# One layer of a diffusion backbone with a mixture of experts on Trainium2: a bias table with memory of its own, one modulation chunk later, a place table ahead of a gate

## The chip, the cores and the metric

The kernel runs on one core of one Trainium2 chip. The metric is device time in microseconds (us), the median of repeated executions. Engines are named as in the profile: PE (TensorE matmul), PEld (its weight load), DVE (VectorE), ACT (ScalarE), POOL (GpSimd), SP (SyncE, which here only issues transfers). A name with q (ACTq, SPq) is an engine's instruction queue.

## The reference

One layer over 256 latent tokens and 256 context tokens of width 1024, all in float32. What matters here:

```python
mod = split((silu(c) @ w_ada + b_ada), 6)                 # w_ada is 1024 x 6144
h = modulate(rms_norm(x), mod[0], mod[1])
y = token_mixing(h, hc, ...) @ w_o                        # windowed GQA and latent attention
x = x + mod[2] * rms_norm(y)
h2 = modulate(rms_norm(x), mod[3], mod[4])
logits = h2 @ w_router + b_router                         # 32 experts, the best 4 of each token
...
gate, lin = split(xb @ w_gate_up[e] + b_gate_up[e], 2)    # 1024 x 2048 per expert
act = (min(gate, 7) * sigmoid(1.702 * gate)) * (clip(lin, -7, 7) + 1)
ys = act @ w_down[e] + b_down[e]                          # 1024 x 1024 per expert
out[token] += weight[token, e] * ys
x = x + mod[5] * rms_norm(out)
```

Every expert's weights are read once: 32 experts of 12 MB.

## The kernel before

The program has three stages. **Projections**: modulation, norms and the input projections. **Attention**: eight units of two heads, written out by hand as a list of calls. **Experts**: a loop over 32 experts. From attention on, each engine carries out its instructions in the order in which the program was written, so a line of that list sets the order on PE, DVE, ACT, POOL and on the queue of SP at once.

*Weight slots.* A slot holds 128 x 2048 float32 (1024 KB). SP loads into slots in a fixed order: the four remaining column groups of `w_ada` in 16 chunks (`ada_load`, L418, source `in_wadr`), `w_o` in four (`load_wo`, L582, `in_wo`), and then 12 slots for each expert (`load`, L743, `in_wexp`): 0 to 3 and 4 to 7 for the two halves of gate and up, 8 to 11 for down. In the expert loop 18 slots take turns. Each transfer signals its landing on one of eight semaphores, which take turns; a transfer may be issued only when the one that used its semaphore before has landed, and when its slot has been read. So about eight transfers are in flight.

*Ada chunks.* `ada(1)` issues the next chunk's load and then does the oldest loaded chunk: two DVE instructions (L431, `accw<-slot,silu,accw`, 128 x 1024) that add two rows of `w_ada`, scaled, to a sum. That chunk's slot is then free for the load. Four chunks make one modulation vector; `accw_106` is the one that the router's shift needs (`column(1)`, L612).

*Attention's calls that the change passes.* `weights(u)` computes scores (L686) and their exponentials (ACT L695); its sums over keys are POOL's (`adds`, L701 and L702, `pa<-pT`). `k_mid` copies keys (ACT L529, L530), `k_flip` transposes them on PE (L536, into the two PSUM buffers `tp`), and each `tp` is split in two: ACT writes the rounded part (L137, `kTm`), DVE the rest (L138, `kTl`). `q_up`, `v_up`, `q_flip` do the same for queries (`qTm`) and values; `v_split` keeps one slot until the last `v_up`. `top_b` finds row maxima (PE L635, DVE L636, `mx`), `values` multiplies by the values (PE L710), `mix(k)` by `w_o` (PE L726, `y`): `mix(0)` and `mix(1)` read what `load_wo(0)` loaded, `mix(2)` and `mix(3)` that of `load_wo(1)`.

*Experts.* Tokens of two experts are gathered by matmuls with a 0/1 table (`take`, PE L995, then `xg`, ACT L1007). `G_(e,c,ks)` multiplies them by half of gate or up (PE L1028, `pw<-slot,xg`; a half in two parts, LOW and HIGH, of two slots each); `T_` transposes the result (PE L1041, `pf`) and makes the activation on DVE and ACT (L1046 to L1053, `actT`); `D_` multiplies by the down weights (PE L1028, `pw<-slot,actT`); `scatter` adds the output to the tokens (PE L1058, `acc`). `place` makes the table that `scatter` uses: two DVE or POOL instructions (L1019, `wo_`), two PE transposes (L1021, `px<-con,wo_`) and an ACT copy (L1022, `ctt`); its `wo_` buffers are single.

*The bias of the down products.* In the loop's turn for expert 30, `bias_rows()` takes a buffer of the tag `xg` (shared with the gathered tokens) and lets ACT issue the load of `b_down` (L1083, `bd<-in_bdn`, 128 KB); `bias_flip` transposes the token weights; and after `G_(31, 0, LOW)`, `bias_add` multiplies the two into the sums (PE L1094, `acc<-bd,wT`, four matmuls). The order there is:

```python
G_(e, 1, HIGH)          # e = 30
bd = bias_rows(); bias_flip(0); bias_flip(1)
G_(31, 0, LOW)
bias_add(0, bd); bias_add(1, bd)
T_(e, 1); G_(31, 0, HIGH); D_(e, LOW); T_(31, 0); D_(e, HIGH)
```

After the last scatter, `finish` normalises, adds and stores the output.

Of the kernel before, what the change touches and what calls it, by code (L numbers as in the profile page):

```python
# [7 lines left out]
F32 = mybir.dt.float32  # L8
# [11 lines left out]
D = 1024  # L20
# [3 lines left out]
E = 32  # L24
# [46 lines left out]
def layer_kernel(ctx, tc, x, cx, cc, wadr, bada, grows, win0, winB, winC, winD, wuqa, wuqb, wukv, wo, wr, wexp, bgu, bgx, bdn, cols, rows, consts, out):  # L71
    nc = tc.nc
    V, S, G, PE = nc.vector, nc.scalar, nc.gpsimd, nc.tensor
# [10 lines left out]
    def wide():  # L84
        return ring.tile([P, 2048], F32, name="slot", tag="wide", bufs=2)
# [50 lines left out]
    def split(hi, lo, src, late=False, eng=V):  # L136
        a = S.copy(hi, src)  # L137
        b = eng.tensor_tensor(lo, src, hi.bitcast(F32), op=ALU.subtract)  # L138
        if late:
            tc.keep_in_program_order(a)  # L140
            tc.keep_in_program_order(b)
# [26 lines left out]
    def ptp(shape=(P, 4, P)):  # L168
        return psb.tile(list(shape), F32, name="tp", tag="tp", bufs=2)
# [240 lines left out]
    def ada_load(pool=None):  # L410
        ch, s = divmod(ada_n[0], 4)
        ada_n[0] += 1
        if s == 0:
            G.memset(accs[ch], 0.0)
            nc.sync.dma_start(accs[ch][0:1], bada[ch:ch + 1])
        w = slot() if pool is None else pool.tile([P, 2048], F32, name="ax", tag="ax", bufs=1)
        w = w.rearrange("p (k c) -> p k c", c=D)
        nc.sync.dma_start(w, wadr[8 + ch * 4 + s].rearrange("p (k c) -> p k c", c=D))  # L418
        ada_q.append((ch, s, w))

    def ada_do(n=1):
        for _ in range(n):
            ch, s, w = ada_q.pop(0)
            a = accs[ch]
            for k in range(2):
                sk = silu[:, 2 * s + k, 0:1]
                if (ch, s, k) in ADA_G:
                    S.activation(w[:, k], w[:, k], AF.Copy, scale=sk)
                    G.tensor_tensor(a, a, w[:, k], op=ALU.add)
                else:  # L430
                    V.scalar_tensor_tensor(a, w[:, k], sk, a, op0=ALU.mult, op1=ALU.add)  # L431
# [95 lines left out]
    def k_mid(i):  # L527
        k96[i] = pqa.tile([P, 8, 96], F32, name="k96", tag="ct", bufs=2)
        S.copy(k96[i][:, :, 0:64], pk[i].rearrange("p (h d) -> p h d", h=8))  # L529
        S.copy(k96[i][:, :, 64:96], krt[:, i][:, None].to_broadcast([P, 8, 32]))  # L530
# [22 lines left out]
    def q_flip(n, t):  # L553
        pt = ptp((96, 4, P))
        for j in range(4):
            PE.transpose(pt[:, j], q96[n, t][:, j], ident)
        split(qTm[n][0:96, 0, t], qTm[n][0:96, 1, t], pt)
# [22 lines left out]
    def load_wo(i):  # L580
        w = wide()
        nc.sync.dma_start(w, wo[i])  # L582
        for k in range(2):
            wov[2 * i + k] = w[:, k * 1024:(k + 1) * 1024]
# [46 lines left out]
    def top_b(h):  # L631
        n, j = divmod(h, 4)
        for t in range(NT):
            s_ = pmm((P, 512))
            PE.matmul(s_, qTm[n][0:96, 0, t, j], kTm[0][n][0:96, j], start=True, stop=True)  # L635
            V.tensor_reduce(mxs[n][:, t, j:j + 1], s_, axis=AX.X, op=ALU.max)  # L636
# [26 lines left out]
    def weights(u):  # L663

        a = u < 4
        pT_[u] = [av.tile([P, 4, T], F32, name="pT", bufs=4) for h in range(2)]
        for g in range(2):
            st = [pmm((P, 2, T)) for h in range(2)]
            for kk in range(2):
                kt = 2 * g + kk  # L670
                ks = slice(kt * P, (kt + 1) * P)
                ops = []
                for h in range(2):
                    if a:
                        k_ = [x_[HALF[h], ks] for x_ in kTg]
                        q_ = [x_[HALF[h], :, u] for x_ in qTg]
                        sl, r = sel[HALF[h], u], rows_["a"][HALF[h]]
                    else:
                        n, j = divmod(2 * (u - 4) + h, 4)
                        k_ = [x_[n][0:96, j, ks] for x_ in kTm]  # L680
                        q_ = [qTm[n][0:96, i, :, j] for i in range(2)]
                        sl, r = sel[0:96, j], rows_[n][0:96]
                    ops.append([(k_[0], q_[0]), (k_[0], q_[1]), (k_[1], q_[0]), (sl, r)])
                for i in range(4):
                    for h in range(2):
                        PE.matmul(st[h][:, kk], *ops[h][i], start=(kk == 0 and i == 0), stop=(i == 3 and not (a and g)),  # L686
                                  skip_group_check=True)
                if a and g:
                    t = 3 - kt
                    for c in range(2):  # L690
                        for h in range(2):
                            PE.matmul(st[h][:, kk, t * P + c * 64:t * P + c * 64 + 64], mask_s[HALF[h], t, c],
                                      ident_b[HALF[h], HALF[h]], start=False, stop=True, skip_group_check=True)
            for h in range(2):
                S.activation(pT_[u][h][:, 2 * g:2 * g + 2], st[h], AF.Exp, scale=A_SCALE if a else B_SCALE)  # L695
        adds(u)
# [34 lines left out]
    tag = {"b0": "big0", "b1": "big1", "d0": "held0", "d1": "held1", "d2": "held2"}  # L731
# [13 lines left out]
    def ada(n):  # L745
        for _ in range(n):
            if ada_n[0] < 16:
                ada_load()
            if ada_q:
                ada_do()  # L750
# [11 lines left out]
    ada(1)  # L762
    weights(0)
    k_mid(0)
    ada(1)
    weights(1)
    k_flip(3)
    k_mid(1)
# [20 lines left out]
    v_up(3)  # L789
    load_wo(0)  # L790
    q_flip(1, 1)
    load_wo(1)
    top_b(0)
    open_y()
# [171 lines left out]
    mo = ctx.enter_context(tc.tile_pool(name="mo", bufs=2, reuse_waits="tile"))  # L966
# [63 lines left out]
    def pw_tile():  # L1030
        return pm.tile([P, 512], F32, name="pw", tag="pw", bufs=2)
# [6 lines left out]
    def flip_z(gu):  # L1038
        pf = pm.tile([P, 4, 2, CAP], F32, name="pf", tag="pf", bufs=1)
        for b in range(4):  # L1040
            PE.transpose(pf[:, b].rearrange("p h c -> p (h c)"), gu[:, b * P:(b + 1) * P], ident)  # L1041
        return pf
# [17 lines left out]
    def act_tile():  # L1060
        return mo.tile([P, KD, CAP], F32, name="actT")
# [6 lines left out]
    def pre(p, eng=G, oh=None):  # L1068
        es = (2 * p, 2 * p + 1)
        g = Gather([(lambda t, e=e: posm[t][:, e:e + 1], lambda t, e=e: wtr[t][:, e:e + 1]) for e in es], eng, oh)  # L1070
        for i, e in enumerate(es):
            gs2[e] = (g, i)
        return g
# [4 lines left out]

    wTs = {}

    def bias_rows():
        bd = mo.tile([E, D], F32, name="bd", tag="xg")
        S.dma_start(bd, bdn)  # L1083
        return bd

    def bias_flip(t):
        px = px_tile().rearrange("p k c -> p (k c)")
# [1 line left out]
        wTs[t] = mo.tile([E, P], F32, name="wT")  # L1089
        V.tensor_copy(wTs[t], px[0:E, 0:P])  # L1090

    def bias_add(t, bd):
        for n in range(2):
            PE.matmul(acc[t][n], wTs[t], bd[:, n * 512:(n + 1) * 512], start=False, stop=False, skip_group_check=True)  # L1094

    g0 = pre(0, V, oh0)
# [41 lines left out]
    def T_(e, c):  # L1138
        if c == 0:
            acts[e] = act_tile()  # L1140
        swiglu(flip_z(gus.pop((e, c))), bg[:, e, c], acts[e], c)

    def D_(e, ks):
        if ks[0] == 0:
            pts[e] = pw_tile()
        gemm(pts[e], wsl(e, 8), lambda k: acts[e][:, k], ks)
        if ks[-1] == KD - 1:
            ys[e] = evict(pts.pop(e), "y")
# [8 lines left out]
    for e in range(E):  # L1157
        loads(12 * e + 12)
        nxt = e + 1 < E
        if e == 0:  # L1160
            G_(0, 1, LOW)
            T_(0, 0)
            G_(0, 1, HIGH)
            G_(1, 0, LOW)
            T_(0, 1)
            G_(1, 0, HIGH)
            g0.place(0)
            D_(0, LOW)
            T_(1, 0)
            g0.place(1)  # L1170
            D_(0, HIGH)
            continue
        g = gs2[e][0] if e % 2 == 0 else pre((e + 1) // 2) if nxt else None
        step = [g.place, g.place] if e % 2 == 0 else [g.take, g.take] if nxt else None
        if step:
            step[0](0)
        G_(e, 1, LOW)
        if step:
            step[1](1)
        if e:  # L1180
            scatter(ys.pop(e - 1), gs2[e - 1][0].ctt[gs2[e - 1][1]], e == 1)
        G_(e, 1, HIGH)
        if e == E - 3:
            count()
        if e == E - 2:
            bd = bias_rows()
            for t in range(NT):
                bias_flip(t)
        if nxt:
            G_(e + 1, 0, LOW)  # L1190
        if e == E - 2:
            for t in range(NT):
                bias_add(t, bd)
        T_(e, 1)
        if nxt:
            G_(e + 1, 0, HIGH)
        D_(e, LOW)
        if nxt:
            T_(e + 1, 0)
        D_(e, HIGH)  # L1200
# [190 lines left out]
```

## Time and profile before

| | |
|---|---|
| median of 3 runs | 1219.4 us (1218.92 to 1219.73) |
| the profiled execution's own time | 1215.98 us |
| its span, first to last instruction | 1214.2 us |
| PE busy | 1107.7 us (91% of the span) |
| DVE, ACT, POOL busy | 306.0, 231.6, 131.7 us |
| moved by DMA | 446.58 MB, 368 GB/s over the span |
| issued loads of expert weights | 384 of 1024 KB, median 19.9 us from issue to landing |
| chain of work that ended last | DMA 64%, PE 30%, DVE 4% of the span |

All times in the rows below are microseconds from the span's start. A busy share over the whole span is a mean over three stages with different limits; which one decides is read stage by stage. A row of the timeline gives start, length, engine, line, operation, output and inputs, the count of instructions merged, and in brackets how long the engine stood idle before it and what ended that.

### The profile page before, as it was taken

How to read it: one execution, taken by the hardware profiler on the slowest of the kernel's cores; microseconds unless marked ns; L12 is line 12 of the kernel's file. 1: busy time of each engine (PE TensorE's matmuls, PEld its weight loads, DVE VectorE, ACT ScalarE, POOL GpSimd, SP SyncE). 2: the span in 40 equal slices, each digit the busy share in tenths (PEclk: the TensorE clock that was granted, in tenths of full speed). 3: DMA queues.
4: the chain of work that ended last, by engine and by line, in shares of the span. 5: the costliest groups of instructions: out<-in, count | busy, mean ns of one | idle time of the engine just before them, and what ended most of it. 6: DMA issues, size and time to landing. Idle time of an engine off the chain costs nothing.

```text
span 1214.2 us, 13597 instructions
## 1 busy us (share of the span) xinstructions
PE 1107.7 (91%) x5441; PEld 474.7 (39%) x5441; DVE 306.0 (25%) x651; ACT 231.6 (19%) x509; POOL 131.7 (11%) x186
## 2 busy tenths in 40 slices
PE   7799899999999999999898989898989898989575
PEld 1587557643343343433232323232323232323121
DVE  3785778431111111121111111111111111111012
ACT  3534412311111111111111111111111111111001
POOL 0301514100101101010101010101010101010000
PEclk9899999899999999999999999999999999999869
DMA  9750386889999999999999999999999999999950
GB/s 380 294 178 1 105 357 232 363 350 420 421 420 420 420 420 420 420 420 420 421 420 421 420 420 420 421 420 419 420 420 421 421 419 421 420 420 421 420 228 36
DMA packets 63194, 446.58 MB, mean 368 GB/s; under 512 B 7284, under 2 KB 7540, under 8 KB 10008
## 3 DMA queue, kind: packets, MB, share of 16 engines
q1 hardware_dynamic: 62648, 444.24, 88.9%
q10 hardware_dynamic: 480, 1.44, 0.4%
q8 instruction: 44, 0.72, 0.2%
q14 instruction: 22, 0.18, 0.0%
HBM read 444.60 MB, written 1.05 MB: 367 GB/s over the span
## 4 chain that ended last, share of the span: by engine, by line
DMA 64%; PE 30%; DVE 4%; ACT 1%; issue 1%; POOL 0%; SPq 0%; POOLq 0%; DVEq 0%; ACTq 0%
DMA slot<-in_wexp 63%; PE pw L1028 11%; PE y L726 2%; PE mm L686 2%; PE mm L274 2%; PE mm L710 1%; PE mm L148 1%; PE mm L146 1%; PE mm L147 1%; PE acc L1058 1%; DVE accw L431 1%; PE px L995 1%; PE pr L547 1%; PE pf L1041 1%; PE acc L1094 1%
## 5 line engine op out<-in xcount | busy, mean ns | idle before, releaser
L1028 PE MATMUL pw<-slot,xg 128*64 128x512 f32 x2048 | 469.5, 601 | 17.5 <-DMA slot<-in_wexp 17.5
L1028 PE MATMUL pw<-slot,actT 128*64 128x512 f32 x1024 | 243.5, 604 | 26.5 <-DMA slot<-in_wexp 25.0
L1028 PEld LDWEIGHTS pw<-slot,xg 128*64 128x64 f32 x2048 | 137.2, 137 | 299.7 <-issue 240.1
L1046 DVE TENSOR_TENSOR z<-pf,bg 128x512 f32<-128x512 f32 x64 | 44.2, 691 | 756.8 <-PE pf L1041 756.8
L1028 PEld LDWEIGHTS pw<-slot,actT 128*64 128x64 f32 x1024 | 69.1, 137 | 176.6 <-issue 104.3
L1050 ACT ACTIVATE sg<-z 128x256 f32<-128x256 f32 x64 | 26.7, 417 | 340.2 <-DVE z L1048 340.2
L1035 ACT COPY gu<-pw 128x512 f32<-128x512 f32 x64 | 37.5, 586 | 229.9 <-PE pw L1028 229.9
L995 PEld LDWEIGHTS px<-oh,xt 128*128 128x128 f32 x480 | 55.8, 191 | 24.3 <-issue 24.3
L1058 PE MATMUL acc<-y,ctt 64*128 64x512 f32 x256 | 63.6, 615 | 0.7 <-ACT y L1035 0.7
L995 PE MATMUL px<-oh,xt 128*128 128x128 f32 x480 | 61.5, 281 | 0.0
L1007 ACT ACTIVATE xg<-px,vcol 128x128 f32<-128x128 f32 x120 | 45.2, 457 | 80.8 <-PE px L995 80.8
L1041 PEld LDWEIGHTS pf<-con,gu 128*128 128x128 f32 x256 | 27.1, 141 | 53.4 <-issue 51.8
L1041 PE MATMUL pf<-con,gu 128*128 128x128 f32 x256 | 42.4, 289 | 0.7 <-ACT gu L1035 0.7
L1035 ACT COPY y<-pw 128x512 f32<-128x512 f32 x32 | 18.8, 586 | 92.5 <-PE pw L1028 89.2
L985 POOL TENSOR_SCALAR oh<-con,posm,r 128x64 f32<-128x64 f32 x60 | 34.0, 586 | 2.5 <-DVE posm L925 2.5
L1052 DVE TENSOR_TENSOR sg<-z,sg 128x256 f32<-128x256 f32 x64 | 27.2, 425 | 18.0 <-ACT sg L1050 18.0
L701 POOL TENSOR_TENSOR pa<-pT 128x512 f32<-128x512 f32 x16 | 23.1, 1447 | 69.3 <-ACT pT L695 54.8
L1058 PEld LDWEIGHTS acc<-y,ctt 64*128 64x128 f32 x256 | 22.0, 186 | 21.8 <-issue 18.4
L726 PE MATMUL y<-slot,of 128*128 128x512 f32 x64 | 30.4, 617 | 0.1
L1053 DVE SCALAR_TENSOR_TENSOR actT<-z,sg 128x256 f32<-128x256 f32 x64 | 27.2, 425 | 2.2
L1094 PE MATMUL acc<-bd,wT 32*128 32x512 f32 x8 | 7.2, 1072 | 21.0 <-DMA bd<-in_bdn 21.0
L274 PE MATMUL mm<-slot,siluz 128*4 128x512 f32 x40 | 19.4, 635 | 7.5 <-DMA slot<-in_wadr 7.5
(449 smaller groups left out, 879.1 us busy)
## 6 DMA issues: line engine op xcount, KB each, us to landing
slot<-in_wexp SPq DMA_DIRECT2D x384, 1024.0 KB, 19.9
slot<-in_wadr SPq DMA_DIRECT2D x20, 1024.0 KB, 7.3
ax<-in_wadr SPq DMA_DIRECT2D x4, 1024.0 KB, 5.8
slot<-in_wo SPq DMA_DIRECT2D x4, 1024.0 KB, 6.3
slot<-in_win SPq DMA_DIRECT2D x2, 1024.0 KB, 9.6
slot<-in_winD SPq DMA_DIRECT2D x2, 768.0 KB, 9.1
slot<-in_winB SPq DMA_DIRECT2D x2, 576.0 KB, 5.5
ct<-in_cx SPq DMA_DIRECT2D x2, 512.0 KB, 10.9
```

The source lines that it names most:

```text
L274: PE.matmul(pad[ch][n], siluz[:, 2 * s + k], w[:, k, n * 512:(n + 1) * 512], start=(s == 0 and k == 0), stop=(last and k == 1), skip_group ...
L726: PE.matmul(y[t][n], oT[k][:, t * P:(t + 1) * P], wov[k][:, n * 512:(n + 1) * 512], start=(k == 0), stop=(k == KD - 1), skip_group_check=True)
L985: eng.tensor_scalar(oh[t][:, i], iota[:, 0:CAP], pos_ap(t), r2[t], op0=ALU.is_equal, op1=ALU.mult)
L995: PE.matmul(px[:, k, 0:ne * CAP], xt[t][:, kk * P:(kk + 1) * P], self.oh[t][:, 0:ne].rearrange("p e c -> p (e c)"), start=(k == 0 and t == ...
L1007: S.activation(o, i, AF.Identity, scale=vcol[:, 1, kk:kk + 1], bias=vcol[:, 0, kk:kk + 1])
L1028: PE.matmul(pt[HALF[h]], lhs(k), wk(k, h), start=(k == 0), stop=(k == KD - 1), skip_group_check=True)
L1035: S.copy(y, pt)
L1041: PE.transpose(pf[:, b].rearrange("p h c -> p (h c)"), gu[:, b * P:(b + 1) * P], ident)
L1046: V.tensor_tensor(z, pf, bias[:, :, :, None].to_broadcast([P, 4, 2, CAP]), op=ALU.add)
L1052: V.tensor_tensor(sg, zg, sg, op=ALU.mult)
L1053: V.scalar_tensor_tensor(actT[:, 4 * c:4 * c + 4], zl, 1.0, sg, op0=ALU.add, op1=ALU.mult)
L1058: PE.matmul(acc[t][n], ctt[HALF[n], t], y[HALF[n]], start=begin, stop=last, skip_group_check=True)
```

## The change

Three edits in the order of the program. The load of `b_down` moves out of the loop to the head of the expert stage, into a tile of its own. One `ada(1)` moves from between `k_mid(0)` and `weights(1)` to between the two `load_wo` calls. In the first expert's turn `g0.place(1)` goes ahead of `T_(1, 0)`.

```diff
     weights(0)
     k_mid(0)
-    ada(1)
     weights(1)
     k_flip(3)
...
     load_wo(0)
     q_flip(1, 1)
+    ada(1)
     load_wo(1)
     top_b(0)
...
-    def bias_rows():
-        bd = mo.tile([E, D], F32, name="bd", tag="xg")
-        S.dma_start(bd, bdn)
-        return bd
+    bd = mo.tile([E, D], F32, name="bd", bufs=1)
+    S.dma_start(bd, bdn)
...
-    def bias_add(t, bd):
+    def bias_add(t):
...
             D_(0, LOW)
+            g0.place(1)
             T_(1, 0)
-            g0.place(1)
             D_(0, HIGH)
...
         if e == E - 2:
-            bd = bias_rows()
             for t in range(NT):
                 bias_flip(t)
```

On DVE in attention, where `k_flip(2)` and then `k_flip(3)` split their transposes, and later where `q_flip(1, 1)` ends and `top_b(0)` begins (rows of before with -, of the change with +):

```order
 L138 TENSOR_TENSOR kTl_1024<-tp,kTm_1022 96x4x128
 L138 TENSOR_TENSOR kTl_1025<-tp,kTm_1023 96x4x128
-L431 SCALAR_TENSOR_TENSOR accw_106<-slot,silu,accw_106 128x1024 x4
+L431 SCALAR_TENSOR_TENSOR accw_106<-slot,silu,accw_106 128x1024 x2
 L138 TENSOR_TENSOR kTl_1024<-tp,kTm_1022 96x4x128
 L138 TENSOR_TENSOR kTl_1025<-tp,kTm_1023 96x4x128
...
 L138 TENSOR_TENSOR qTm_1027<-tp,qTm_1027 96x512 x2
+L431 SCALAR_TENSOR_TENSOR accw_106<-slot,silu,accw_106 128x1024 x2
 L636 TENSOR_REDUCE mx<-mm 128x1 x4
 L431 SCALAR_TENSOR_TENSOR accw_107<-slot,silu,accw_107 128x1024 x2
```

Two of the four chunk instructions ahead of the second `kTl` pair now stand ahead of the first row maxima. On the queue of SP the chunk loads keep their number, but the second of the two loads that stood ahead of the `w_o` loads now stands between them:

```order
 L418 DMA slot<-in_wadr 128x2048 x2
 L415 DMA accw_107<-in_bada 1x1024
-L418 DMA slot<-in_wadr 128x2048 x2
-L582 DMA slot<-in_wo 128x2048 x2
+L418 DMA slot<-in_wadr 128x2048
+L582 DMA slot<-in_wo 128x2048
+L418 DMA slot<-in_wadr 128x2048
+L582 DMA slot<-in_wo 128x2048
 L418 DMA slot<-in_wadr 128x2048
 L743 DMA slot_1571<-in_wexp 128x2048
```

On ACT at the head of the expert stage, now (bg is the table of the gate and up biases; in brackets the semaphores that an instruction waits for, DMAHW0 to DMAHW7 being the eight of the transfers):

```order
L888 COPY h2T_2035<-mm 128x512 [waits PE_49]
L971 DMA bg<-in_bgu 128x512 [waits DMAHW7_49,PE_49]
L1082 DMA bd<-in_bdn 32x1024 [waits DMAHW5_49,DMAHW0_49]
L1007 ACTIVATE xg<-acc_2229,vcol 128x128 [waits PE_49]
L1007 ACTIVATE xg<-acc_2229,vcol 128x128 x3
```

and before, in the turn of expert 30:

```order
L1035 COPY gu<-pw 128x512 [waits PE_49,Activation_49]
L1083 DMA bd<-in_bdn 32x1024 [waits DMAHW6_49]
L1050 ACTIVATE sg<-z 128x256 [waits DVE_49]
L1035 COPY gu<-pw 128x512 [waits PE_49,Activation_49]
```

The load of bd went from behind an eviction of expert 30 to behind the load of bg, ahead of the first gathered tokens.

## Rows read from the trace of the kernel before

**Rows 1.** Windows: length, busy PE, PEld, DVE, ACT, POOL; PE clock; DMA share; GB/s.

```profile
252.00:257.00 5.00, 5.00 (x26) 1.59 (x24) 2.80 (x13) 0.81 (x5) 0.00 (x0) 1.00 0.64 221
...
264.00:371.00 107.00, 104.24 (x504) 39.45 (x500) 17.12 (x45) 17.96 (x41) 9.11 (x16) 0.98 1.01 421
...
371.00:1135.00 764.00, 719.78 (x3410) 261.50 (x3410) 106.85 (x266) 115.35 (x261) 57.87 (x101) 1.00 1.01 420
...
1135.00:1165.00 30.00, 8.63 (x28) 2.82 (x25) 0.56 (x2) 0.59 (x1) 0.00 (x0) 0.65 1.01 413
```

**Rows 2.** The chain that ended last: start, length, what.

```profile
1135.86 19.87 DMA slot<-in_wexp
...
1155.74 5.64 DMA bd<-in_bdn
...
1200.73 0.02 issue
```

**Rows 3.** The same windows view, the microsecond in which the transfers end.

```profile
1173.00:1174.00 1.00, 1.00 (x6) 0.33 (x4) 0.00 (x0) 0.00 (x0) 0.00 (x0) 0.50 0.02 8
```

**Rows 4.** Timeline of PE round the bias matmuls.

```profile
1136.77 3.65 PE L1028 MATMUL pw<-slot,xg 128*64 128x512 f32 x16
...
1161.43 7.19 PE L1094 MATMUL acc<-bd,wT 32*128 32x512 f32 x8 [21.00 <-DMA bd<-in_bdn]
...
1169.59 6.17 PE L1028 MATMUL pw<-slot,xg 128*64 128x512 f32 x16
...
1179.12 0.66 PE L1041 MATMUL pf<-con,gu 128*128 128x128 f32 x4
...
1186.72 1.99 PE L1058 MATMUL acc<-y,ctt 64*128 64x512 f32 x8
```

**Rows 5.** Timeline of DVE, ACT and PE in attention.

```profile
121.36 7.38 DVE L431 SCALAR_TENSOR_TENSOR accw<-slot,silu,accw 128x1024 f32<-128x1024 f32 x4
...
125.11 1.12 ACT L137 CAST kTm<-tp 96x512 fp32r<-96x512 f32 x2
...
129.40 1.53 PE L536 MATMUL tp<-con,k 128*96 128x128 f32 x8 [4.35 <-DVE kTl L138]
...
130.86 3.29 PE L710 MATMUL mm<-pT,vg 128*64 128x256 f32 x16
...
143.73 1.95 PE L710 MATMUL mm<-pT,vg 128*64 128x256 f32 x16
```

**Rows 6.** The windows view, two microseconds of attention behind a wait of PE.

```profile
132.00:134.00 2.00, 2.00 (x14) 1.07 (x12) 0.27 (x1) 0.00 (x0) 0.00 (x0) 0.59 0.45 184
```

**Rows 7.** Timeline of DVE where the chunk goes.

```profile
166.41 1.29 DVE L636 TENSOR_REDUCE mx<-mm 128x1 f32<-128x512 f32 x2 [1.97 <-PE mm L635]
...
167.62 2.60 DVE L431 SCALAR_TENSOR_TENSOR accw<-slot,silu,accw 128x1024 f32<-128x1024 f32 x2
...
173.25 2.48 DVE L636 TENSOR_REDUCE mx<-mm 128x1 f32<-128x512 f32 x4 [0.91 <-PE mm L635]
```

**Rows 8.** Timeline of SP's queue and of PE, loads and use of w_o.

```profile
154.65 1.01 SPq L582 DMA_DIRECT2D slot<-in_wo  x2
...
161.46 0.33 SPq L418 DMA_DIRECT2D slot<-in_wadr  x1
...
175.80 3.68 PE L726 MATMUL y<-slot,of 128*128 128x512 f32 x8
```

**Rows 9.** Timeline of PE in the first expert's turn.

```profile
280.13 0.30 PE L1021 MATMUL px<-con,wo__2403 128*128 128x128 f32 x1 [2.76 <-DVE wo__2403 L1019]
...
280.52 5.27 PE L1028 MATMUL pw<-slot,actT 128*64 128x512 f32 x16
```

**Rows 10.** Timeline of ACT's and SP's queues at the expert stage's head.

```profile
203.94 17.87 SPq L743 DMA_DIRECT2D slot<-in_wexp  x10
...
246.06 0.34 ACTq L971 DMA_DIRECT2D bg<-in_bgu  x1
...
250.64 1.51 ACT L1007 ACTIVATE xg<-acc,vcol 128x128 f32<-128x128 f32 x4 [8.46 <-PE acc L995]
```

More of the change, by code (lines that the diff above doesn't have):

```diff
@@ L1192, in layer_kernel @@
             for t in range(NT):
-                bias_add(t, bd)
+                bias_add(t)
         T_(e, 1)
```

## The prediction

> **What bounds the kernel now.** I read the windows by stage first. From 264 to 1165 us the transfers run at 413 to 421 GB/s with a DMA share of 1.01, in every stretch [rows 1]; just ahead of that, at 252 to 257, they reach 221 GB/s. A slot of 1,048,576 bytes takes 2.5 us at 420 GB/s. So from 264 on the stream of weights is full: when it ends is settled by when it became full and by the bytes left. PE follows it: in 371 to 1135 it is busy 719.78 of 764.00 us and waits for weights the rest. The reader should see that a faster PE buys nothing there.
>
> Next I read the end of the chain of waits. It leaves the weights at 1155.72, when one load lands; at once ACT issues the load of bd, which takes 5.64 us, and from its landing on the chain is PE's [rows 2]. The timeline of PE shows what that is: PE ends a gate half at 1140.42, stands idle for 21.00 us until bd is there, and then needs 7.19 us for the bias matmuls [rows 4], while the stream goes on at 413 GB/s [rows 1]. Finer windows show the stream's end: 8 GB/s in 1173 to 1174 [rows 3], so the last slot landed at about 1173.9. The last down matmul ends at 1200.73 [rows 2] and the span at 1214.2: PE ends 27 us behind the weights. Those 27 us are the price of one wait.
>
> **Term 1, bd's wait.** ACT's last work ahead of that issue is an eviction of a half that PE had done before 1136.77, so ACT stood some 19 us in front of it. It waited for nothing but a landing semaphore (DMAHW6 in the program's order), which bd's transfer shares with a weight load eight transfers earlier; the buffer was free. Now the load stands at the head of the stage, so PE goes straight on at 1140.4. What then bounds the end is either PE's own work or the last landing.
>
> PE's own work from 1140.4 to the last slot: the bias matmuls at the higher clock, 7.19 / 2 = 3.6 us (after the wait PE ran at the lower level: 16 matmuls took 6.17 us and not 3.65 [rows 4]); seven further half products of 3.6 us (25.2), less the last slot's half of one (1.8); a scatter of 1.99, three transposes of 0.66 and a short wait for an eviction (4.5 together) [rows 4]. Sum 31.5 us, so 1171.9. The last slot lands at 1173.9, and the slots before it every 2.5 us ahead of that. So PE is 2 us ahead of the stream, waits for it as in the 764 us before, and ends its last slot 1.9 us after the landing, at 1175.8. From there to the span's end everything is as before, 1214.2 - 1200.7 = 13.5 us: 1189.3. **Term 1: -24.9 us**. If the 2 us of lead were not there (say PE needs 4 us more than I sum) it would be -22 to -23.
>
> Side costs: bd's 128 KB leave the full stream, 0.13 MB at 420 GB/s = **-0.3 us**. They come back at 246.4, where the stream is not full (221 GB/s at 252 to 257): nothing. The issue on ACT is like that of bg, 0.34 us, and ACT then stands idle 8.46 us until 250.64 [rows 10]: hidden. If that cover were gone, it would cost 0.34 us on the gathered tokens.
>
> **Term 2, the ada chunk in attention.** DVE does two chunks back to back, 7.38 us from 121.36. ACT has rounded the keys for `k_flip(3)` at 125.11 plus 1.12, in two pieces, but DVE gets to its part of the split only at 128.7, and PE, which needs those PSUM buffers back, stands for 4.35 us until 129.40 [rows 5]. With one chunk there DVE is free at about 125.0, so the first split can run at 125.7 (ACT's first piece) for 0.65 us, and PE goes on at about 126.4: -3.0 us. Behind the long wait PE runs at the lower level: granted 0.59 in 132 to 134 [rows 6], and 16 value matmuls take 3.29 us where the next unit's take 1.95 [rows 5]. A wait of 1.4 us is shorter than the two behind which these rows show a drop (4.35 here, 2.76 in rows 9), so I take the higher level: another -1.3. The bounds of this term are 0 (something else holds PE there) and -4.4; I take **-4.3**, near the upper one, since all of PE's next inputs (exponentials, POOL's sums, keys) are older than 127.
>
> At its new place the chunk costs DVE 2.60 us, as the next one at 167.62 does, ahead of the first row maxima. What is queued behind it: those maxima, which free two of the four score buffers, then a unit's reciprocal. DVE stands idle there 1.97 us before 166.41 and 0.91 us before 173.25 [rows 7], 2.88 in all, so it has caught up by `top_b(2)`: nothing, with 2.6 us as the other bound.
>
> The Trainium skill, in "SBUF — State Buffer", section "Who interferes with whom", says that a DVE instruction with two SBUF inputs contends with a GpSimd instruction that reads SBUF. The trace agrees: 7.38 us for four beside POOL's sums, 2.60 for two elsewhere. By that rule the chunk is cheap at its new place as long as POOL has no sums there; at the dearer price it would be 3.7 us, 0.8 more than the slack, and the sum 0.8 us poorer.
>
> The transfers that it moves: the chunk's load now stands between the two `w_o` loads and waits for the slot that `v_split` held, which before was free at 161.46. So `load_wo(1)`, before at about 155.3, comes at 161.5 less the 4.3 gained, 157.2, and lands some 7 us later, 164; its first use is `mix(2)`, before at 175.80 [rows 8], then 171.5. Covered by 7 us. The expert loads behind it on SP's queue (first at about 161.8) come no earlier, and are not needed then.
>
> From there the gain goes on to the stream: the loads from 203.94 on are issued as PE and DVE free slots, and the gap at 252 to 257 is a lack of free slots; if PE reaches the first gate 4.3 us earlier, the stream is full 4.3 us earlier and ends 4.3 us earlier.
>
> **Term 3, the place table.** PE waits 2.76 us for DVE, which makes an activation first and the table second, and then runs 16 matmuls in 5.27 us [rows 9] and not in 3.65 [rows 4]. With the table ahead, DVE has long made it, so PE saves 2.76 + 1.62 = 4.4 us at 277 to 286. But the stream is full there (264 to 371: 421 GB/s, rows 1); PE only catches up with it sooner than 371. **Nothing.**
>
> **Sum.** -24.9 - 0.3 - 4.3 = -29.5 us. The profiled execution took 1215.98 us (its span and 1.8 around it): 1186.5. The median of the three runs is 3.4 us above it, so I add the sum to that: 1219.4 - 29.5 = **1189.9 us**.
>
> **Rivals.**
>
> *A: the chunk buys nothing.* Its DVE time is only moved, and row maxima or the lower clock take the gain back further on. For it: DVE has one chunk more between two waits that are hardly longer than it [rows 7], and where PE's clock drops in attention can shift. Against: the slack of 2.88 us. Only term 1 and bd's bytes stay: 1219.4 - 25.2 = 1194.2.
>
> *B: the place table pays in full.* The chain of waits runs through PE from 264 to 371, so a PE wait removed there would shorten it. 1189.9 - 4.4 = 1185.5. Against it: transfers at 421 GB/s throughout. The Trainium skill speaks for this one: "Perfetto Trace Analysis", section "Optimization Strategies", wants the engine that keeps PE waiting to be served first. The row that decides here is the full stream, which that rule leaves out.
>
> *C: PE itself ends behind the stream.* The bias matmuls and the transposes come on top of an ordinary turn, and if my sum of 31.5 us is 6 short, PE ends 4 us late: 1193.9. Against it: PE's rate in 371 to 1135.
>
> *D, the other side: bd holds ACT.* Its issue now stands ahead of the gathered tokens on ACT's queue and waits for the landing of one weight load. If that landed late, PE's first gate would wait, no slot would come free, and the stream would be full later, us for us. It turns the result when ACT is held for 29 us beyond 250.64, until about 280; then 1219 or more. Against it: the load in question is one of ten issued from 203.94 to 221.81 [rows 10], and with eight in flight at 2.5 us it has landed by 242, before bg is issued at 246.06.
>
> *E: bd still waits at the end.* Then only term 2 is left, 1215. Against it: PE's bias matmuls would have to wait for a load issued 900 us earlier.
>
> **How the numbers follow.** My forecast 0.68; A 0.15, B 0.06, C 0.07, D 0.02, E 0.02. The time is the forecast's, 1190. Its own range is 1187 to 1192, from term 2's bounds and the clock. To hold eight in ten it takes in A, C and half of B: 1185.5 to 1195.5. A measurement of this kernel can tell about 0.2% (2.4 us) from no change; all but D are faster by more than that: faster 0.97, same 0.01, slower 0.02.
>
> **What would show it.** After: no idle time in front of the bias matmuls, and those in about 3.6 us; the chain's last change from weights to PE within 2 us of the last landing, and that landing 4 to 5 us earlier than 1173.9; PE's wait in front of the second `k_flip` under 2 us and no lower clock behind it; PE's wait at the second place table gone while the transfers in 264 to 371 stay at 421 GB/s; bd's issue next to bg's. I would be wrong if the last landing does not move (A), moves by 9 us (B), if the last down product starts well behind it (C), or if the first gate starts later than 250.5 (D).

## The result, and the profile after

The changed kernel takes **1191.2 us** (median of 4 runs, 1190.33 to 1191.56); the kernel before took 1219.5 us beside it (4 runs). The ratio is 0.9768, 95% interval [0.9751, 0.9785]: 28.3 us less (26.2 to 30.4). 1189.9 was predicted, 29.5 less. The profiled execution of after took 1190.33 us, its span is 1188.5 us.

The end first. The chain of waits of after, in 1150 to 1175 us; it answers to [rows 2], where a load of bd and the bias matmuls stood:

```profile
1151.99 21.04 DMA slot<-in_wexp
1173.02 0.04 issue
1173.07 1.96 PE pw L1028 x8
```

In this stretch the chain passes from the stream of weights to PE once, at the landing of the last slot, and PE then has 1.96 us of products and an end like before's: from the last landing to the end of the span are 15.5 us (1188.5 - 1173.0), where before it was 40.3 (1214.2 - 1173.9). That is 24.8 us.

The timeline of PE of after at the bias matmuls and at the last slot, beside [rows 4]:

```profile
1135.64 3.65 PE L1028 MATMUL pw<-slot,xg 128*64 128x512 f32 x16
1139.22 3.69 PE L1092 MATMUL acc<-bd,wT 32*128 32x512 f32 x8
1142.85 1.09 PE L1041 MATMUL pf<-con,gu 128*128 128x128 f32 x4
1143.87 4.86 PE L1028 MATMUL pw<-slot,xg 128*64 128x512 f32 x16
1148.56 3.60 PE L1028 MATMUL pw<-slot,actT 128*64 128x512 f32 x16
...
1173.07 1.94 PE L1028 MATMUL pw<-slot,actT 128*64 128x512 f32 x8 [0.43 <-DMA slot<-in_wexp]
```

The row of the bias matmuls has no bracket: nothing was waited for, and they take 3.69 us and not 7.19. A short stretch at the lower clock follows (4.86 us where the next sixteen take 3.60), and PE is still in time: at the last slot it waits for the stream, 0.43 us.

The stages in windows, beside [rows 1, 3] (columns: length, busy time of PE, PEld, DVE, ACT, POOL, granted clock, DMA share, GB/s):

```profile
252.00:257.00 5.00, 5.00 (x26) 1.60 (x24) 2.78 (x13) 0.39 (x2) 0.00 (x0) 1.00 0.74 287
264.00:371.00 107.00, 107.00 (x524) 40.67 (x522) 17.18 (x44) 18.34 (x42) 10.43 (x18) 1.00 1.01 420
371.00:1135.00 764.00, 716.99 (x3391) 259.68 (x3387) 106.94 (x266) 115.07 (x261) 56.59 (x98) 1.00 1.01 420
1172.00:1173.00 1.00, 0.64 (x4) 0.00 (x0) 0.00 (x0) 0.00 (x0) 0.00 (x0) 1.00 0.02 8
```

In 264 to 371 PE is now busy without a gap (107.00 us, before 104.24), and the transfers move the same 420 GB/s. The last bytes fall in 1172 to 1173, one window earlier than before and not the four or five that were forecast.

Attention, on PE, from the k_flip ahead of the moved chunk to the first gate:

```profile
126.18 1.08 PE L536 MATMUL tp<-con,k 128*96 128x128 f32 x8
128.73 1.24 PE L536 MATMUL tp<-con,k 128*96 128x128 f32 x8 [1.47 <-DVE kTl L138]
129.90 1.95 PE L710 MATMUL mm<-pT,vg 128*64 128x256 f32 x16
...
171.69 1.95 PE L612 MATMUL mm<-con,accw 128*128 128x1 f32 x16
173.50 5.38 PE L726 MATMUL y<-slot,of 128*128 128x512 f32 x8
...
250.06 6.23 PE L1028 MATMUL pw<-slot,xg 128*64 128x512 f32 x28
```

PE waits 1.47 us where [rows 5] show 4.35, and the value matmuls behind it take 1.95 and not 3.29. But the eight `w_o` matmuls at 173.50 take 5.38 us; in before the same eight took 3.68. And the first k_flip stands at 126.18, in before at 123.97: this execution was 2.2 us late before it came to any edit. So the first gate starts 0.47 us earlier, not four.

The chunk at its new place, on DVE, beside [rows 7]:

```profile
160.87 2.59 DVE L431 SCALAR_TENSOR_TENSOR accw<-slot,silu,accw 128x1024 f32<-128x1024 f32 x2
163.38 2.48 DVE L636 TENSOR_REDUCE mx<-mm 128x1 f32<-128x512 f32 x4
```

It costs the cheap 2.59 us, and the row maxima follow at once.

### The profile page after: what moved, and what is told of

Same layout as the page of the kernel before. It is cut to its first block, busy times and chain, and to the rows that moved or that the text cites. A ratio compares the mean times of both kernels' runs of the same rounds, so it can differ in the third digit from the quotient of the medians.

```text
span 1188.5 us, 13594 instructions
## 1 busy us (share of the span) xinstructions
PE 1103.8 (93%) x5441; PEld 473.1 (40%) x5441; DVE 306.5 (26%) x651; ACT 231.6 (19%) x509; POOL 133.0 (11%) x186
## 4 chain that ended last, share of the span: by engine, by line
DMA 68%; PE 26%; DVE 3%; ACT 1%; issue 1%; POOL 0%; SPq 0%; POOLq 0%; ACTq 0%; DVEq 0%
DMA slot<-in_wexp 67%; PE pw L1028 8%; PE y L726 2%; PE mm L274 2%; PE mm L686 2%; PE mm L710 1%; PE mm L148 1%; PE mm L146 1%; PE mm L147 1%; PE acc L1058 1%; PE pr L547 1%; PE px L995 1%; DMA slot<-in_wadr 0%; PE pf L1041 0%; ACT pT L695 0%
## 5 line engine op out<-in xcount | busy, mean ns | idle before, releaser
L1052 DVE TENSOR_TENSOR sg<-z,sg 128x256 f32<-128x256 f32 x64 | 27.2, 426 | 18.1 <-ACT sg L1050 18.1
L726 PE MATMUL y<-slot,of 128*128 128x512 f32 x64 | 31.6, 636 | 0.1
L1053 DVE SCALAR_TENSOR_TENSOR actT<-z,sg 128x256 f32<-128x256 f32 x64 | 27.2, 425 | 2.2
L124 POOL TENSOR_TENSOR rstd<-rstd,mh 128x1 f32<-128x1 f32 x14 | 10.7, 767 | 131.3 <-DVE rstd L121 127.5
```

What stands on the lines that cost most here:

```text
L726: PE.matmul(y[t][n], oT[k][:, t * P:(t + 1) * P], wov[k][:, n * 512:(n + 1) * 512], start=(k == 0), stop=(k == KD - 1), skip_group_check=True)
L1052: V.tensor_tensor(sg, zg, sg, op=ALU.mult)
L1053: V.scalar_tensor_tensor(actT[:, 4 * c:4 * c + 4], zl, 1.0, sg, op0=ALU.add, op1=ALU.mult)
```

## The experiments

Twelve runs on three chips. Before's own median differs by chip (1215.7, 1216.0, 1217.3 us), so every difference is taken against before on the same chip: the microseconds given are that median times what the ratio lacks to one.

### One edit at a time, on the kernel before

**bd's edit alone.**

```diff
+    bd = mo.tile([E, D], F32, name="bd", bufs=1)
+    S.dma_start(bd, bdn)          # head of the experts' stage
...
-            bd = bias_rows()      # turn of expert 30
```

> Term 1 alone: bd gets memory of its own and its load stands at the head of the experts' stage; chunk and place table stay as before. If the forecast's term 1 and the bytes are right: 1219.4 - 24.9 - 0.3 = 1194.2 us (1192.5 to 1196 with the clock's scatter), no idle time in front of the bias matmuls, PE's end some 15.5 us behind the last landing. Rival C (PE's own work is then the end): 1197 or more. Rival E (bd still waits): 1219.4. If the three edits need one another: anything well away from 1194.

Measured: 1191.3 us against 1215.7, ratio 0.9801 [0.9788, 0.9814]: **-24.2 us** (22.6 to 25.8). The timeline of PE of this kernel:

```profile
1136.16 3.65 PE L1028 MATMUL pw<-slot,xg 128*64 128x512 f32 x16
1139.75 3.69 PE L1092 MATMUL acc<-bd,wT 32*128 32x512 f32 x8
```

No wait in front of the bias. Term 1 stands, by itself and at nearly its size; E is out.

**The chunk alone.**

```diff
     k_mid(0)
-    ada(1)
     weights(1)
...
     q_flip(1, 1)
+    ada(1)
     load_wo(1)
```

> Term 2 alone: the ada chunk at its later place in attention's order, bd and the place table as before. The forecast (4.3 us gained in attention come through to the end, since the stream is full that much earlier): 1215.1 us. If part of it is lost again at about 175 us, where the trace after shows a lower clock that before did not have: 1216.5 to 1217.5. Rival A (the chunk buys nothing): 1219.4.

Measured: 1213.5 us (9 runs), ratio 0.9974 [0.9963, 0.9986]: **-3.2 us** (1.7 to 4.5; the medians alone lie 2.3 us apart). The timeline of PE of this kernel:

```profile
124.31 1.08 PE L536 MATMUL tp<-con,k 128*96 128x128 f32 x8
126.86 1.24 PE L536 MATMUL tp<-con,k 128*96 128x128 f32 x8 [1.47 <-DVE kTl L138]
...
171.63 5.38 PE L726 MATMUL y<-slot,of 128*128 128x512 f32 x8
...
248.22 8.37 PE L1028 MATMUL pw<-slot,xg 128*64 128x512 f32 x37
```

From the first of these rows to the gate are 123.91 us; in before, 126.56 (250.53 - 123.97). So 2.65 us of PE's time are gained, and the 5.38 of the changed kernel is here too: the lower clock at 172 us comes with the chunk's move, not with the other edits. A is out: its zero lies outside the interval. The forecast's 4.3 lies inside it, so that less came through is shown by the distances in the traces and not by the times.

**The place table alone.**

```diff
             D_(0, LOW)
+            g0.place(1)
             T_(1, 0)
-            g0.place(1)
```

> Term 3 alone: the place table ahead of the second expert's gate half. The forecast (the stream of weights is full there): 1219.4 us, with PE's wait in front of the second place matmuls gone and PE 4 to 5 us earlier from 280 us on, the last landing unmoved. Rival B (it pays in full): 1215.0, with the last landing 4.4 us earlier.

Measured: 1215.9 us, ratio 1.0002 [0.9993, 1.0011]: **nothing**. The timeline of PE and a window of this kernel, beside [rows 9] and the row of 264 to 371 in [rows 1]:

```profile
276.13 0.33 PE L1021 MATMUL px<-con,wo__2389 128*128 128x128 f32 x1
...
276.94 3.65 PE L1028 MATMUL pw<-slot,actT 128*64 128x512 f32 x16
280.52 2.05 PE L995 MATMUL px<-oh,xt 128*128 128x128 f32 x16
```

```profile
264.00:371.00 107.00, 107.00 (x526) 40.76 (x524) 17.18 (x44) 18.34 (x42) 10.43 (x18) 1.00 1.01 420
```

The wait of 2.76 us is gone and the matmuls behind it run at the higher clock, and none of it reaches the end. B is out. The rule of the Trainium skill beside it ("Perfetto Trace Analysis", section "Optimization Strategies": where PE waits for other engines, speed up those that block the critical path) found no gain here. The chain of waits of before did run through this wait, from the activation on DVE at 277.40 to the table's transposes at 280.13; the stream was already full, and the measurement decides.

### What held bd

**Memory of its own, the load at its old place** (on the kernel before).

```diff
+    bd = mo.tile([E, D], F32, name="bd", bufs=1)
     def bias_rows():
-        bd = mo.tile([E, D], F32, name="bd", tag="xg")
         S.dma_start(bd, bdn)
```

> Half of bd's edit: memory of its own, but its load is issued at the old place, in the turn before the last. If a landing semaphore shared with a weight load is what held the load (the prediction's reading): nothing gained, 1219.4 us, ACT held in front of the issue for some 19 us and PE idle for some 21 us in front of the bias matmuls. Rival (the buffer shared with xg is what it waited for, so memory of its own is the cure): 1194.2 us and no idle time there.

Measured: 1215.7 us, ratio 1.0003 [0.9994, 1.0012]: nothing gained. The timeline of ACT, and that of PE:

```profile
1136.16 0.59 ACT L1035 COPY gu<-pw 128x512 f32<-128x512 f32 x1 [5.19 <-PE pw L1028]
1155.61 0.34 ACTq L1084 DMA_DIRECT2D bd<-in_bdn  x1
...
1136.86 3.65 PE L1028 MATMUL pw<-slot,xg 128*64 128x512 f32 x16
1161.26 7.19 PE L1094 MATMUL acc<-bd,wT 32*128 32x512 f32 x8 [20.74 <-DMA bd<-in_bdn]
```

ACT is done at 1136.75 and issues 18.9 us later. With nobody else in bd's buffer, that can't be the buffer. The chain of waits of this run has a weight load that ends at 1155.59 (1135.74 + 19.85), and the issue follows it by 0.02 us.

**Memory of its own, ACT issues it in the middle of the stream** (on the changed kernel).

```diff
-    S.dma_start(bd, bdn)          # head of the experts' stage
...
         G_(e, 1, HIGH)
+        if e == 10:
+            S.dma_start(bd, bdn)
```

> On the changed kernel: bd keeps memory of its own, but ACT issues its load in turn 10 of the experts, in the middle of the full stream. If the landing semaphore holds it: ACT stands some 19 us in front of the issue in turn 10 and PE some 15 to 20 us behind it, but the stream stays full from the slots that are free and PE, which needs some 2.4 us less than the stream for each expert, catches up over the next turns: 1191.2 us as before this edit, within 1. Rival 1 (so long a stop of PE runs the ring of slots dry and the stream pauses): later by up to 20 us, 1195 to 1210. Rival 2 (the hold belongs to the last turns alone): ACT is not held at turn 10.

Measured: 1189.6 us, ratio 0.9778 [0.9757, 0.9799], like the changed kernel. The timeline of ACT and of PE, and windows of this kernel:

```profile
532.93 0.59 ACT L1035 COPY gu<-pw 128x512 f32<-128x512 f32 x1 [5.19 <-PE pw L1028]
557.36 0.34 ACTq L1181 DMA_DIRECT2D bd<-in_bdn  x1
557.75 0.42 ACT L1050 ACTIVATE sg<-z 128x256 f32<-128x256 f32 x1 [24.23 <-DMA slot<-in_wexp]
...
558.69 1.12 PE L1041 MATMUL pf<-con,gu 128*128 128x128 f32 x4 [11.82 <-ACT gu L1035]
```

```profile
545.00:555.00 10.00, 1.87 (x8) 0.41 (x8) 0.00 (x0) 0.00 (x0) 0.00 (x0) 0.84 1.01 420
555.00:565.00 10.00, 6.31 (x24) 2.58 (x25) 2.88 (x7) 1.66 (x4) 0.00 (x0) 0.65 1.01 397
565.00:600.00 35.00, 35.00 (x176) 13.88 (x176) 4.07 (x10) 6.47 (x16) 4.59 (x8) 1.00 1.01 421
```

The hold is no matter of the last turns: ACT stands for 24 us in the middle of the stream, and what the trace names at its end is the landing of a weight load. PE stands for 11.8 us behind it. It costs nothing measurable, because the stream goes on at 397 to 421 GB/s into free slots (SP issues 24 loads from 519.98 to 578.46), and PE, busy without a gap from 565 on, catches up. The same hold in turn 30 cost some 24 us: behind it PE has no turns left to catch up in.

**Memory of its own, SP issues it in turn 29** (on the changed kernel).

```diff
-    S.dma_start(bd, bdn)          # head of the experts' stage
...
         loads(12 * e + 12)
+        if e == E - 3:
+            nc.sync.dma_start(bd, bdn)
```

> On the changed kernel: bd keeps memory of its own, and SP issues its load in turn 29, among the weight loads. If what cost the time before was that ACT stood in front of the issue and that bd landed last: no engine but SP is held, bd lands a few us behind the weight loads ahead of it and long before turn 30's bias matmuls; 0.13 MB more in the full stream is 0.3 us: 1191.5 us. Rival (a small load in the full stream is itself late by 20 us or more): PE idle again in front of the bias matmuls, 1195 to 1212.

Measured: 1190.0 us, ratio 0.9791 [0.9776, 0.9805]. The timelines of SP and PE:

```profile
1104.70 0.33 SPq L1157 DMA_DIRECT2D bd<-in_bdn  x1
...
1140.36 3.70 PE L1091 MATMUL acc<-bd,wT 32*128 32x512 f32 x8
```

The load may stand late and inside the full stream, if it is a turn ahead of its use and the engine that waits for the semaphore is one for which nobody waits. An early place is one cure, as bd's edit alone shows. SP's queue is a second; here it came together with an earlier turn, and no run separates the two.

The Trainium skill ("DMA: Bandwidth & Descriptors", section "Anatomy of one DMA — SWDGE (gpsimd) path") says, in a section on transfers that GpSimd issues, that the DMA engines do not wait on semaphores and that any such wait is done by the sequencer that issues, ahead of dispatch. Two traces agree for transfers that ACT issues: 18.9 and 24 us in which ACT stood in front of its issue.

### What else could set the end of the changed kernel

**The chunk loaded at its new place, its sum left out.**

```diff
     q_flip(1, 1)
-    ada(1)
+    ada_load()
+    ada_q.pop(0)
     load_wo(1)
```

> On the changed kernel: the ada chunk at its new place is loaded, but DVE's sum over it is left out, so the output lacks that part of the scale. It measures what the chunk's DVE time costs at its new place. The forecast (slack of 2.88 us covers it): 1191.2 us, within 0.7. Rival A (the later place takes the gain back): up to 2.6 us less, 1188.6. If the chunk's time shifts the lower clock at about 175 us as well: 1.7 us less, 1189.5.

**The bias left out.**

```diff
-    bd = mo.tile([E, D], F32, name="bd", bufs=1)
-    S.dma_start(bd, bdn)
...
-        if e == E - 2:
-            for t in range(NT):
-                bias_flip(t)
...
-        if e == E - 2:
-            for t in range(NT):
-                bias_add(t)
```

> On the changed kernel: the bias of the down product is left out altogether (its load, the transposes of the gates' weights and the eight matmuls), so the output lacks that bias. If the last landing sets the end and PE's bias work is hidden in front of it, as the forecast has it: only bd's 0.13 MB is left out of a stream that is not full there, 1191.0 us, within 0.7. Rival C (PE's own work sets the end): 3.7 to 6 us less, 1185.5 to 1187.5.

Measured beside the two runs above, on one chip: 1189.3 us without the chunk's sum (ratio 0.9786 [0.9772, 0.9800]) and 1188.9 without the bias (0.9785 [0.9772, 0.9799]); the kernels that have both took 1189.6 and 1190.0. So 2.6 us less DVE work at the chunk's new place, or 3.7 us less PE work ahead of the last slots, is worth under 1.1 us by medians (each interval is some 1.7 us to either side): both are hidden, as forecast, and C, at 3.7 us or more, is out as the rule. The `w_o` matmuls without the chunk's sum:

```profile
170.11 1.95 PE L612 MATMUL mm<-con,accw 128*128 128x1 f32 x16
171.91 5.38 PE L726 MATMUL y<-slot,of 128*128 128x512 f32 x8
```

So the lower clock there doesn't come from DVE's time either.

### The lower clock at 172 us

Four kernels on one chip: the changed kernel again, the changed kernel with the chunk at its old place, and two with line 612 edited.

> The changed kernel itself once more, beside the three others on one chip, so that they can be compared with it. Its time stood 28.3 us below before's: 1188 us where before takes 1216, ratio 0.9768 within its interval.

> The changed kernel with the ada chunk back at its old place in attention: edits one and three without edit two. If terms 1 and 3 are as forecast and the chunk's move is worth what its own run showed (3.2 us): 3.2 us above the changed kernel of this call. By the prediction's term 2 as written: 4.3 us above it. Rival A (the chunk buys nothing): equal to it within 1. If the place table pays once bd no longer ends the kernel: below the run with bd's edit alone, 24.2 us under before, by up to 4.4 us.

Measured: 1190.9 us and 1194.8 us; ratios 0.9763 [0.9739, 0.9787] and 0.9806 [0.9786, 0.9825]. In the full change too the chunk's move has its worth, 3.9 us by medians and 5.2 by the ratios, whose intervals just touch. The place table is again worth nothing (0.9806 here, 0.9801 with bd's edit alone, on another chip).

```diff
-        pcol[ch] = p_ = pmm((P, KD))
+        c_ = 64 if ch == 1 else 1            # second kernel: 64 for both
+        px_ = pmm((P, KD, c_))
         for k in range(KD):
-            PE.matmul(p_[:, k:k + 1], accs[ch][:, k * P:(k + 1) * P], ones_f[:, 0:1], ...)
+            PE.matmul(px_[:, k], accs[ch][:, k * P:(k + 1) * P], ones_f[:, 0:c_], ...)
+        pcol[ch] = p_ = px_[:, :, 0]
```

> On the changed kernel: the sixteen matmuls with one moving column at line 612 for the first of two uses (at 171.7 us of the changed kernel's trace) get 64 equal columns instead of one; the same sums. If what PE does there brings the lower clock granted right behind it, which took eight w_o matmuls from 3.68 us in before to 5.38 us: no lower clock at 173 to 177 us, and, since the stream starts that much earlier, 1.7 us below the changed kernel of this call. Rival (the lower clock comes from something earlier, or from none of PE's work): 5.38 us stay, no change.

> The same at both uses of line 612, the second at 208.1 us of the changed kernel's trace, behind which the granted clock is 0.5 at 211.1 to 217.9 us. If both lower stretches are brought by these matmuls: 1.7 us and, at half speed over the second stretch of 6.8 us, some 2.5 to 3.4 us: 4.2 to 5.1 us below the changed kernel of this call, and the first gate that much earlier. Rival (the clock falls elsewhere instead): no gain, with lower stretches at other places. Rival (wider matmuls cost PE more than the clock gives back): later by the longer matmuls, up to 2 us each.

Measured: 1185.5 us both, ratios 0.9747 [0.9724, 0.9769] and 0.9742 [0.9723, 0.9762]. The timeline of PE with the first use widened:

```profile
124.81 1.08 PE L536 MATMUL tp<-con,k 128*96 128x128 f32 x8
...
170.31 2.00 PE L613 MATMUL mm<-con,accw 128*128 128x64 f32 x16
172.14 3.65 PE L728 MATMUL y<-slot,of 128*128 128x512 f32 x8
...
244.42 10.52 PE L1030 MATMUL pw<-slot,xg 128*64 128x512 f32 x48
```

Sixty-four columns cost PE 0.05 us more than one, and the 5.38 us are 3.65. Since the time from the k_flip ahead of the moved chunk to the first gate is free of what an execution loses earlier, it sets nine of the profiles side by side (from the rows of PE, at lines 536 and 1028, or their counterparts in kernels with other line numbers):

| kernel | k_flip | first gate | between | L726 behind column(1) | clock in 212 to 216 |
|---|---|---|---|---|---|
| before | 123.97 | 250.53 | 126.56 | 3.68 | 0.52 |
| change, chunk at its old place | 128.28 | 255.45 | 127.17 | 3.68 | 1.00 |
| chunk alone | 124.31 | 248.22 | 123.91 | 5.38 | 0.50 |
| changed kernel | 126.18 | 250.06 | 123.88 | 5.38 | 0.50 |
| changed kernel again | 128.21 | 252.14 | 123.93 | 5.38 | 0.71 |
| chunk's sum left out | 124.61 | 248.34 | 123.73 | 5.38 | 0.50 |
| bias left out | 123.80 | 243.41 | 119.61 | 3.68 | 1.00 |
| column(1) wide | 124.81 | 244.42 | 119.61 | 3.65 | 1.00 |
| both wide | 125.79 | 245.40 | 119.61 | 3.65 | 1.00 |

(With the chunk at its old place, in the full change, the second lower stretch lies at 217 to 224, behind the window of the last column. The five profiles that the table leaves out agree: 126.56, 126.58 and 126.77 between the two rows with the chunk at its old place, 123.93 and 123.86 with it moved.) Three levels stand out: 126.6 to 127.2 with the chunk at its old place, 123.9 with it moved, 119.6 where neither lower stretch comes. So a further 4.3 us lay behind the change. Whether the wide columns are what gives them back is not settled: the kernel without bias has narrow ones and had neither stretch in its profile (that execution took 1183.9 us, its five others 1188 to 1190), and widening the first use alone also cleared the second stretch, which stands behind matmuls left as they were. The times lean to them: 1184.2 to 1189.4 and 1184.7 to 1188.5 us, against 1186.1 to 1193.8 for the changed kernel on that chip. The medians lie 5.4 us lower; the intervals of the ratios overlap, and two of the five executions with the first use widened took 1188.9 and 1189.4 us at a lower mean clock than the other three (0.987 and 0.988 against 0.990 and 0.991). What brings the lower clock at 172 us stays open.

## Why the prediction was right, point by point

**Term 1, -24.9 and -0.3: right.** Measured alone, -24.2 (22.6 to 25.8) where 25.2 was forecast; the end behind the last landing is shorter by 24.8 in the profiles. The cause was right as well: the landing of a weight load held ACT's issue, and not the buffer (the two runs with memory of its own on ACT). PE is ahead of the stream at the last slot, but by 0.43 us and not by the 2 of the sum, which left out a stretch at the lower clock (4.86 us for sixteen matmuls and not 3.65); leaving out the bias gains nothing more. In the changed kernel's second profile, an execution of 1193.75 us, that stretch was twice as long (1145.5 to 1152.3), the same sixteen matmuls took 6.16 us, and the chain ran through PE from 1130 on. That is rival C, in one execution, at under 1 us: the last weight load was issued at 1155.1 and landed 20.4 us later, at 1175.5, and from there to the span's end (1191.8) are 16.3 us, against 15.5.

**Term 2, -4.3: right in mechanism, too large.** The steps came as written: the wait 1.47 us (1.4 predicted), no lower clock behind it, the new place free. Up to the `w_o` matmuls behind `column(1)` even 4.5 us were gained (from the k_flip 173.50 - 126.18 = 47.32 us, before 175.80 - 123.97 = 51.83). The step that was mis-sized is "From there the gain goes on to the stream": on the way, at 172 to 177 us, 1.7 us were lost (5.38 - 3.68) to a lower clock that before did not have there. -4.3 + 1.7 = -2.6; the time to the first gate says -2.65. The runs say -3.2 alone and -3.9 to -5.2 within the change, too coarsely to tell 2.65 from 4.3. Why the clock falls there is not shown. I had put that under rival A ("where PE's clock drops in attention can shift") and given it only whole, as the loss of the full gain. A term for a part of it was missing.

**Term 3, nothing: right**, twice measured.

**The sum.** -24.2 - 3.2 + 0.2 = -27.2 us from the three edits alone, -28.3 measured together, -29.5 predicted: the edits add up within their intervals. The forecast's sign "that landing 4 to 5 us earlier" didn't come in the one pair of profiles (0.9 us), because the profiled execution of after was 2.2 us late before any edit. The ends of a single pair of profiles are too coarse for a gain of 3 us; nine runs told it from nothing, and the distance between two rows of one trace told its size.

**The rivals.** A is excluded by the chunk's own run, and the run with the chunk at its old place speaks against it; B is excluded by two runs, E by bd's edit alone; D did not happen: ACT issues bd at 246.01, right behind bg, and the gate starts at 250.06.

## What to carry to other kernels

A small load that an engine of the critical path issues late in a full stream is dear for its issue, not for its bytes: look at what the issuing instruction waits for, and give it an early place, or, a turn ahead of its use, a queue for which nobody waits. The same stop costs nothing as long as the stream goes on and PE has turns left to catch up in; it costs all of itself at the end. For gains of a few microseconds compare the distance between two rows inside each trace, on both sides of the edit, and not the ends of two executions.

## What the runs showed of the hardware

Executions differ by what they lose early: in the nine profiles of the table the k_flip starts anywhere from 123.80 to 128.28 us, in code that no edit touched, and in the two of the changed kernel at 126.18 and 128.21; what it is lost to was not followed up.

The lower clock comes at few and repeated places: behind long waits, behind the sixteen one-column matmuls, and behind the eight bias matmuls, where PE had not stood still (in six of the nine profiles in which bd is there in time, the sixteen matmuls next behind them took 4.83 to 6.16 us, in the other three 3.65). The stretches go together: with the chunk moved the one behind the 4.35 us wait is gone, and in six of seven profiles with narrow columns one stands at 172 us instead. In those six a second one follows some 40 us on, at 212; in the three profiles with the chunk moved that lack the one at 172 (without the bias, and the two with wide columns) the second is missing too.

The Trainium skill ("TensorE: Matmul & The Clock Gate", section "What's actually happening") says that how many matmuls run at the lower clock, at the start of one and the same kernel, varies from run to run. The two profiles of the changed kernel show such a difference at its end: 4.86 and 6.16 us for the same sixteen matmuls.

Matmuls with 64 moving columns take nearly what those with one take (2.00 against 1.95 us for sixteen).
